# A hybrid attention layer: the first two output tiles' turned planes loaded a step earlier and ahead of their gate rows, and two weight pieces split in one step

## The chip, the cores and the metric

The kernel runs on one core of a Trainium2 chip. What counts is the device time of one launch in microseconds (us). The engines are TensorE (PE; PEld is its weight load), VectorE (DVE), ScalarE (ACT), GpSimd (POOL) and SyncE (SP), which here only issues transfers.

## What is computed

```python
h = rms_norm(x, g_pre) * (1 + scale) + shift          # x: 2048 x 1024, f32
qa, ka, va, fa, za, qb, kb, vb, zb = split(h @ w_in)
oa = forgetting_attention(qa, ka, va, fa + b_fgate)    # 8 heads of 64, causal, with a cumulative gate bias
oa = oa * silu(za)
ob = sliding_window_sink_attention(rope(qb), rope(kb), vb, sinks) * silu(zb)
y = concatenate([oa, ob]) @ w_out                      # 1024 x 1024
out = x + gate * rms_norm(y, g_post)
```

The gate, scale and shift come from `silu(c) @ w_ada + b_ada`.

## The kernel before

Matrix products keep f32 accuracy with f16 operands: each operand is split into a high and a low half, and three matmuls (high x high, high x low, low x high) make one product.

After the projections and the sliding-window branch, the kernel goes through the eight heads of the forgetting attention (`hd` 0 to 7), with 20 steps each (`r` 0 to 19). A step is two key blocks against one chunk of 512 queries; the four chunks take 2, 4, 6 and 8 steps. Step `r` does, in this order: `exp32` on ScalarE (L1354); a tick; `low` of the step before on VectorE (L1365); half of the filler work on TensorE; its own `high` on ScalarE (L1362); the scores of the next step on TensorE (L1349, L1350); a second tick; `pv`, the product with the values of step `r - 2`, on TensorE (L1375 to L1378); the other half of the filler. On the last step of a chunk, `pv` also empties its accumulator on VectorE (L1382, L1384), and some ticks later the result is stored in DRAM as `o_d` (L1388, on SyncE's queue). POOL clears the masked part of diagonal blocks (L1358).

The program order is written out by hand: every engine and every queue works its own instructions in the order in which the code issues them, and waits where data is missing. `after(n, f)` puts `f` off by `n` ticks, so two ticks are one step.

In the last head (`hd` 7) the filler is first the rest of the gate projection (L335, whose results go to `z_d` in DRAM by L378 and L386), and from `r` 11 on the output product. For this product:

- `w_out_load(m)` loads one of 16 pieces of `w_out` (128x512 f32, 256 KB, L1459); `w_out_split(m)` makes its high half (ScalarE L1465 or POOL L1467), `w_out_low(m)` its low half (VectorE L1471). `w_at` says in which step a piece is split; it is loaded three steps before.
- `Out(t)` is an output tile of 128 rows, t = 0 to 15. `load_o` reads the attention planes (high and low half) from `o_d`, turned by the DMA engine (two transposes, L1487), `load_z` the gate rows from `z_d` (512 KB, L1493). Tile t uses the slots `t % 2` of one buffer.
- `turn(lag)` registers a tile's chain: `join` adds the planes (VectorE, L1505, tile `osum`), `gate` multiplies by the gate rows (VectorE, L1509), `squares_` (ScalarE, L1512), `scale_` sums them over partitions on TensorE (L1516) and makes a scale (VectorE, L112, L113), then the high half (ScalarE, L1523) and the low half (VectorE, L1526, tile `oz`) of the product's operand.
- `product` does three matmuls of a unit (L1542). Units come in the order tile 0, tile 1 on the first 512 columns, both on the second, then tiles 2 to 15. Tiles 0 to 3 are partly done between the steps of the last head; the rest of the product runs alone, from step 19's end to the end of the kernel.
- When both column halves of a tile are done, VectorE and ScalarE normalise (L1550, L1564, L92 to L106, L1602) and POOL's queue stores the rows (L1603).

Of the kernel before, what the change touches and what calls it, by code (L numbers as in the profile page):

```python
# [40 lines left out]
def hybrid_layer(  # L41
# [38 lines left out]
    def sm(n, tag):  # L80
        return small.tile([P, n], F32, tag=tag, name=tag)
# [27 lines left out]
    def root_scale(dst, ss):  # L109

        h = small.tile([P, 1], I32, tag="rs_h", name="sc_h")
        V.tensor_scalar(h[:], ss.bitcast(I32), 1, None, op0=ALU.logical_shift_right)  # L112
        V.tensor_scalar(dst.bitcast(I32), h[:], -1, 0x5F3759DF + (15 << 23), op0=ALU.mult, op1=ALU.add)  # L113
# [57 lines left out]
    def bank(hold=False):  # L171
        n = next(n for n in order_ if n not in held)
        order_.remove(n)
        order_.append(n)
        if hold:
            held.add(n)
        return n
# [8 lines left out]
    lag = [0]  # L186

    def after(n, f):
        late.append([n, f])

    def tick():
        now = [f for n, f in late if n <= 1]
        late[:] = [[n - 1, f] for n, f in late if n > 1]
        for f in now:
            f()
# [227 lines left out]
    def turn(ci, k):  # L423

        px = ps_x.tile([P, CH], F32, tag="x", name="px")
        for u in range(4):
            PE.transpose(px[:, u * P:(u + 1) * P], xt[ci * 4 + u][:, k * P:(k + 1) * P], ident[:])
        hf = hst.tile([P, CH], F32, tag="hf", name="hf")
        hi, lo = hT[ci][:, 0, k, :], hT[ci][:, 1, k, :]

        high = k % 2 == 0 if ci else k in (0, 4)

        def scaled():
            for dst in ([hi] if high else []) + [hf[:]]:
                A.activation(dst, px[:], AF.Identity, scale=Gp[:, k:k + 1], bias=Shp[:, k:k + 1])

        def split():
            if not high:
                V.tensor_copy(hi, hf[:])
            V.tensor_tensor(lo, hf[:], hi, op=ALU.subtract)  # L440

        return scaled, split
# [673 lines left out]
    def tick2():  # L1116
        cnt[0] += 1
        if cnt[0] % 2 == 0:
            tick()
# [354 lines left out]
    class Out:  # L1474
# [20 lines left out]
        def turn(self, lag):  # L1495

            self.hl = wpool.tile([P, 2, KT, P], F16, tag=("whl", "wraw")[self.t % 2], name="oz")
            self.sc = sm(1, "w_pw")
            hi, lo = self.hl[:, 0], self.hl[:, 1]
            gs = sm(1, "w_mx")  # L1500

            c = oio["c"]

            def join():
                V.tensor_tensor(c, self.o[:, 0], self.o[:, 1], op=ALU.add)  # L1505
                self.joined = True

            def gate():
                V.tensor_tensor(self.z, c, self.z, op=ALU.mult)  # L1509

            def squares_():
                A.activation(oio["j"][0].rearrange("p (k n) -> p k n", k=KT), self.z, AF.Square, accum_out=gs[:])  # L1512

            def scale_():
                pg = bk[bank()][:, 0:1]
                PE.matmul(pg, ones[:], gs[:], start=True, stop=True)  # L1516
                root_scale(self.sc[:], pg)

            after(1, join)
            after(2 if lag > 4 else 1, gate)  # L1520
            after(3 if lag > 4 else 2, squares_)
            after(lag, scale_)
            after(lag + 1, lambda: A.activation(hi, self.z, AF.Copy, scale=self.sc[:]))  # L1523

            def low():
                V.scalar_tensor_tensor(lo, self.z, self.sc[:], hi, op0=ALU.mult, op1=ALU.subtract)  # L1526
                self.turned = True

            after(lag + 2, low)
# [75 lines left out]
    outs = [Out(t) for t in range(NB)]  # L1605
# [32 lines left out]
    with tc.manual_schedule():  # L1638
        mi = 0
        V.memset(cmask[:], 0.0)  # L1640
        V.tensor_copy(cmask[:, 3 * P:], dmask[:])
        for n in range(2):
            for slot in (2, 0):
                const_rows(n, slot)
                tick()
        fill(8, tick2)
        key_limbs(0)
        key_rows(0)
        tick()
        while pos[0] < N_V3 or mi < M_LEAD:  # L1650
            if pos[0] < N_V3:
                fill(1)
            if mi < M_LEAD and pos[0] >= N_QK0 - 10:
                munits[mi]()
                mi += 1
            tick2()
        for _ in range(3):
            tick()
        steps[0].scores()
        p0, p_one = pos[0], len(punits) - P_LAST - 8  # L1660
        p_tot = p_one + 16 - p0 - P_LEAD
        m_ramp, m_from, m_done = 0, 6 * NS + 7, 7 * NS + 3

        w_at = {3: [0], 4: [1], 5: [2], 6: [3], 7: [4], 8: [5], 10: [6], 11: [7], 12: [8], 13: [9], 14: [10, 11],
                15: [12, 13], 16: [14], 17: [15]}
        w_all = sum(s.w for s in steps[:7 * NS])
        w_acc = 0
        lag[0] = 4
        for s, stp_ in enumerate(steps):
            hd, r = divmod(s, NS)  # L1670
            w_acc += stp_.w
            npn = p0 + P_LEAD + p_tot * w_acc // w_all
            npn = min(npn, (npn + p_one) // 2) - pos[0]
            fil = fill
            if hd == 7:
                npn = len(punits) - P_LAST + min((P_LAST * (r + 1) + 10) // 11, P_LAST) - pos[0]
            if hd == 7 and r > 10:
                npn, fil = N_IN * (r - 10) // (NS - 11) - opos[0], ofill
            m_goal = M_LEAD + int(round((s + 1) * M_HEAD / NS))
            if s == m_from:  # L1680
                m_ramp = mi
            if s >= m_from:
                m_goal = m_ramp + (len(munits) - m_ramp) * (s + 1 - m_from) // (m_done + 1 - m_from)
            m_goal = min(len(munits), m_goal)
            todo = []
            nmn = m_goal - mi
            a = b = 0
            while a < npn or b < nmn:
                if b >= nmn or (a < npn and a * nmn <= b * npn):
                    todo.append(lambda: fil(1))  # L1690
                    a += 1
                else:
                    todo.append(munits[mi + b])
                    b += 1
            mi = m_goal
            half = (len(todo) + 1) // 2
            if r == 2 and hd + 1 < 8:
                key_limbs(hd + 1)
            if hd == 7 and r:
                for m in w_at.get(r + 3, []):  # L1700
                    w_out_load(m)
            stp_.exp32()
            tick()
            if s:
                steps[s - 1].low()
            if hd == 7:
                for m in w_at.get(r, []):
                    w_out_split(m)
            for u in todo[:half]:
                u()  # L1710
            stp_.high()
            if s + 1 < len(steps):
                steps[s + 1].scores()
            tick()
            if s >= PV_LAG:
                steps[s - PV_LAG].pv()
            if hd == 7:
                for m in w_at.get(r, []):
                    w_out_low(m)
            for u in todo[half:]:  # L1720
                u()
            if r == 3 and hd + 1 < 8:
                key_rows(hd + 1)
            if hd == 7 and r == 0:
                open_out()
            if hd == 7 and r == 0:
                for m in w_at[3]:
                    w_out_load(m)
            if hd == 7 and r in (4, 5):
                outs[r - 4].load_z()  # L1730
            if hd == 7 and r in (6, 7):
                outs[r - 6].load_o()
            if hd == 7 and r in (7, 9):
                outs[(r - 7) // 2].turn(5)
            if s % 4 == 1 and s // 4 <= 32:
                w_square(s // 4)
            if s == 134:
                w_sum()
            if s == 136:
                w_root()  # L1740
            if s % 8 == 2 and s // 8 < KT + 2:
                gate_load(s // 8)
            if s % 8 == 7 and s // 8 < KT + 2:
                gate_use(s // 8)
        assert pos[0] == len(punits) and mi == len(munits) and opos[0] == N_IN and not events
        tick()
        steps[-1].low()
        for n in range(PV_LAG, 0, -1):
            steps[-n].pv()
        tick()  # L1750
        tick()
        fxs.close()
        ofill(len(ounits) - opos[0], tick2)
        for _ in range(4):
            tick()
# [35 lines left out]
```

## Time and profile before

| what | us |
|---|---|
| median of 3 runs | 1145.53 |
| lowest, highest | 1144.94, 1145.73 |
| the profiled execution | 1143.33 |
| its span, first to last instruction | 1141.6 |
| busy in it: TensorE, VectorE, ScalarE, POOL | 1101.9, 936.1, 691.8, 252.7 |
| its mean granted TensorE clock | 0.995 of full |

The profile is of one execution; its times are from the start of the span. A row of a timeline gives start, duration, engine, line, operation, result and operands with their shapes, and in brackets how long the engine had been idle and what ended that. A row of waits gives who waited for whom, us in total, times, and the longest. A row of the chain that ended last gives start, duration and what. The mapping of rows to steps follows from the order above: the exponent of step 9 of the last head, for example, is the L1354 at 936.88 us.

### The profile page before, as it was taken

Reading aid. Unit: us, or ns where it says so; the run is one execution under the profiler, and the core shown is the slowest. Engines: PE = TensorE matmul, PEld = TensorE weight load, DVE = VectorE, ACT = ScalarE, POOL = GpSimd, SP = SyncE. Lnnn points to the kernel's source line nnn. Section 1 sums busy time; section 2 is a strip of 40 time slices with the busy share of each in tenths; the row PEclk is TensorE's granted clock in tenths of the full one; section 3 lists DMA queues with packets and bytes.
Section 4 is the critical chain, followed back from the end, with each engine's and each line's share of the span. In section 5 each row is a group of like instructions: output and inputs, shape, how many; then the busy total and the mean of one; then the engine's idle time right before and its main releaser. Section 6 shows DMA issues by size and latency. Waiting matters only on the chain. (4 is left out here: it accounts for less than half of the span.)

```text
span 1141.6 us, 26966 instructions
## 1 busy us (share of the span) xinstructions
PE 1101.9 (97%) x10386; PEld 637.4 (56%) x10386; DVE 936.1 (82%) x2331; ACT 691.8 (61%) x1177; POOL 252.7 (22%) x391
## 2 busy tenths in 40 slices
PE   5899999999999999999999999999999998999997
PEld 1466657654569955555555555555555554544443
DVE  6775668879899658889898889978888988888885
ACT  4676446656666534767767677777777777433331
POOL 2011122434443311122221221202111136100000
PEclk9999999999999999999999999999999999999999
DMA  9646436676787532243332432223212168478753
GB/s 332 225 139 170 105 72 138 113 157 127 158 163 139 115 66 70 68 104 74 81 78 66 103 84 62 59 57 80 61 38 58 25 169 221 133 187 217 189 164 111
DMA packets 210324, 136.35 MB, mean 119 GB/s; under 512 B 145276, under 2 KB 189348, under 8 KB 210196
## 3 DMA queue, kind: packets, MB, share of 16 engines
q1 hardware_dynamic: 198100, 98.53, 37.2%
q0 software_dynamic: 11616, 35.58, 11.0%
q8 instruction: 81, 1.33, 0.5%
q10 hardware_dynamic: 480, 0.53, 0.2%
q14 instruction: 47, 0.39, 0.1%
HBM read 62.58 MB, written 25.18 MB: 77 GB/s over the span
## 5 line engine op out<-in xcount | busy, mean ns | idle before, releaser
L1354 ACT ACTIVATE p<-sta,lift,scl_qk 128x1024 f32<-128x1024 f32 (+2 forms) x160 | 171.8, 1074 | 80.3 <-PE sta L1350 75.8
L335 PE MATMUL bk<-hT,wh_qk 128*128 128x512 f16 x768 | 198.0, 378 | 0.0
L1542 PE MATMUL bk<-hT,oz 128*128 128x512 f16 (+2 forms) x792 | 169.7, 372 | 2.4 <-DVE hT L1471 1.4
L1365 DVE TENSOR_TENSOR pha<-p,pha 128x1024 f16<-128x1024 f32 (+2 forms) x160 | 171.3, 1071 | 0.0
L1362 ACT ACTIVATE pha<-p 128x1024 f16<-128x1024 f32 (+2 forms) x160 | 148.2, 926 | 33.6 <-POOL p L1358 30.0
L1303 DVE TENSOR_REDUCE a_m<-bk 128x1 f32<-128x512 f32 x192 | 129.0, 683 | 33.2 <-PE bk L1300 32.9
L1542 PEld LDWEIGHTS <-oz 128*128 128x128 f16 x792 | 75.9, 99 | 87.7 <-issue 1.7
L1375 PE MATMUL poa<-vt,pha 128*128 128x65 f16 x1088 | 117.2, 193 | 2.1 <-DVE ona L1384 2.1
L1378 PE MATMUL poa<-vt,pha 128*128 128x65 f16 x1088 | 116.6, 193 | 1.8 <-DVE pha L1365 1.7
L1377 PE MATMUL poa<-vt,pha 128*128 128x64 f16 x1088 | 117.0, 195 | 0.0
L1349 PE MATMUL sta<-T 128*128 128x512 f16 (+1 forms) x320 | 109.8, 348 | 3.9 <-ACT p L1354 3.9
L1375 PEld LDWEIGHTS <-pha 128*128 128x128 f16 x1088 | 101.9, 97 | 16.5 <-DVE ona L1384 2.9
L1300 PE MATMUL bk<-T 66*128 66x512 f16 (+2 forms) x320 | 110.2, 348 | 0.8 <-DVE a_m L1305 0.5
L1377 PEld LDWEIGHTS <-pha 128*128 128x128 f16 x1088 | 101.4, 97 | 13.6
L335 PEld LDWEIGHTS <-wh_qk 128*128 128x128 f16 x768 | 70.2, 97 | 69.4 <-issue 0.6
L1350 PE MATMUL sta<-T 69*128 69x512 f16 (+1 forms) x320 | 108.2, 348 | 0.0
L1378 PEld LDWEIGHTS <-pha 128*128 128x128 f16 x1088 | 101.2, 99 | 2.1 <-DVE pha L1365 2.1
L335 PE MATMUL bk<-hT,wh_za 128*128 128x512 f16 x384 | 100.2, 380 | 0.0
L353 PE MATMUL bk<-wh_va,hT 128*128 128x128 f16 x1536 | 92.6, 219 | 0.0
L1358 POOL TENSOR_SCALAR_AFFINE_SELECT p<-p 128x256 f32<-128x256 f32 x64 | 34.7, 542 | 254.9 <-ACT p L1354 234.7
L335 PE MATMUL bk<-hT,wh_zb 128*128 128x512 f16 x384 | 90.8, 379 | 0.0
L353 PEld LDWEIGHTS <-hT 128*128 128x128 f16 x1536 | 87.5, 98 | 4.9 <-issue 2.5
(504 smaller groups left out, 1952.4 us busy)
## 6 DMA issues: line engine op xcount, KB each, us to landing
hT<-in_x_dram SPq DMA_DIRECT2D x20, 512.0 KB
wa<-in_w_ada_dram SPq DMA_DIRECT2D x16, 512.0 KB
T<-stq SPq DMA_DIRECT2D x128, 64.0 KB
T<-z_d SPq DMA_DIRECT2D x16, 512.0 KB
out_dram<-hT POOLq DMA_DIRECT2D x15, 512.0 KB, 5.7
z_d<-tz POOLq DMA_DIRECT2D x29, 256.0 KB, 3.1
xt<-in_x_dram SPq DMA_DIRECT2D x12, 512.0 KB
qs<-qf SPq DMA_DIRECT2D x80, 64.0 KB
```

The costliest lines, as they stand in the source:

```text
L335: PE.matmul(ps, whl[:, a, k, :], hT[ci][:, b, k, :], start=(k == 0 and n == 0), stop=(k == KT - 1 and n == 2))
L353: PE.matmul(ps[:, u * P:(u + 1) * P], hT[ci][:, a, k, u * P:(u + 1) * P], whl[:, b, k, :], start=(k == 0 and n == 0), stop=(k == KT - 1 an ...
L1300: PE.matmul(mx[:, :w], T[0:XM, 0, i * P:(i + 1) * P], T[0:XM, 2, pc * CH:pc * CH + w], start=True, stop=True)
L1303: V.tensor_reduce(m3[:, u, pc:pc + 1], mx[:, :w], axis=AX.X, op=ALU.max)
L1349: PE.matmul(self.st[:, o:o + w], T[:, 3, kb_], T[:, 1, qc], start=True, stop=False)
L1354: A.activation(self.p32[:, :self.w], self.st[:, :self.w], AF.Exp, scale=scl[f"qk{self.hd}"][:], bias=lift[:])
L1362: A.activation(self.ph[:, 0, :self.w], self.p32[:, :self.w], AF.Copy)
L1365: V.tensor_tensor(self.ph[:, 1, :self.w], self.p32[:, :self.w], self.ph[:, 0, :self.w], op=ALU.subtract)
L1375: PE.matmul(po[:, u, :], ph[:, 0, pq], vt[:, b, hd, 0:65], start=(self.first and n == 0 and u == 0), stop=False)
L1377: PE.matmul(po[:, u, 0:64], ph[:, 0, pq], vt[:, b, hd, 65:VW], start=False, stop=False)
L1378: PE.matmul(po[:, u, :], ph[:, 1, pq], vt[:, b, hd, 0:65], start=False, stop=(self.last and n == len(self.blocks) - 1))
L1542: PE.matmul(py, self.hl[:, i, k, :], w_piece(8 * j + k, cc), start=(k == 0 and m_ == 0), stop=(k == KT - 1 and m_ == 2))
```

## The change

In the last head the planes of tiles 0 and 1 (`load_o`) are issued at the end of steps 5 and 6 instead of 6 and 7. Their gate rows (`load_z`) move from steps 4 and 5 to 5 and 6, behind the planes. `turn` is called at the end of steps 6 and 8 instead of 7 and 9, with lag 6 instead of 5. Counted in ticks after that call, the chain is now: join 1, gate 2, squares 4, scale 6, high half 7, low half 8; it was 1, 2, 3, 5, 6, 7. So tile 0's join goes from the first tick of step 8 to the first of step 7, its low half from the first tick of step 11 to the second of step 10. Later tiles call `turn(7)`; their order is unchanged.

Piece 15 of `w_out` is split in step 16, with piece 14, instead of step 17. `w_from` keeps every load where it was.

```diff
             after(1, join)
-            after(2 if lag > 4 else 1, gate)
-            after(3 if lag > 4 else 2, squares_)
+            after(2, gate)
+            after(4 if lag == 6 else 3, squares_)
             after(lag, scale_)
...
         w_at = {3: [0], 4: [1], 5: [2], 6: [3], 7: [4], 8: [5], 10: [6], 11: [7], 12: [8], 13: [9], 14: [10, 11],
-                15: [12, 13], 16: [14], 17: [15]}
+                15: [12, 13], 16: [14, 15]}
+        w_from = {m: (13 if m == 14 else 14 if m == 15 else r - 3) for r, ms in w_at.items() for m in ms}
...
             if hd == 7 and r:
-                for m in w_at.get(r + 3, []):
+                for m in (m for m, at in w_from.items() if at == r):
                     w_out_load(m)
...
-            if hd == 7 and r in (4, 5):
-                outs[r - 4].load_z()
-            if hd == 7 and r in (6, 7):
-                outs[r - 6].load_o()
-            if hd == 7 and r in (7, 9):
-                outs[(r - 7) // 2].turn(5)
+            if hd == 7 and r in (5, 6):
+                outs[r - 5].load_o()
+                outs[r - 5].load_z()
+            if hd == 7 and r in (6, 8):
+                outs[(r - 6) // 2].turn(6)
```

## The prediction

> **What bounds the kernel now.** I read the page first (busy shares, the chain that ended last), then the waits between 880 and 990 us, then each engine's timeline there.
>
> ```profile
> PE 1101.9 (97%) x10386; PEld 637.4 (56%) x10386; DVE 936.1 (82%) x2331; ACT 691.8 (61%) x1177; POOL 252.7 (22%) x391
> ...
> 987.38 12.97 PE bk L1542 x60
> ...
> DVE osum L1505 <- DMA T<-o_d: 2.7, 1, 2.7
> PE poa L1378 <- DVE pha L1365: 1.7, 2, 1.4
> PE sta L1349 <- ACT p L1354: 1.7, 2, 0.9
> PE bk L1542 <- DVE hT L1471: 1.4, 1, 1.4
> PE bk L1542 <- DVE oz L1526: 0.7, 1, 0.7
> ```
>
> TensorE is the bound. From 987.38 us (second line, from the chain) it streams the output product with nothing to wait for, and no line of that stretch is edited. So the change is worth exactly what it shifts that 987.38. Before it, the four TensorE waits shown come to 5.5 us. The first line, VectorE's 2.7 us for the turned planes, comes ahead of all but the one for L1471.
>
> **The first two tiles' chain: when do the planes land?** This is SyncE's queue, in order. L1388 stores the last head's first rows to o_d, L1493 loads a gate tile (512 KB), L1459 a w_out piece (256 KB), L1487 the two transposes of a tile (start, duration of the issue).
>
> ```profile
> 927.60 0.40 SPq L1388 DMA_DIRECT2D o_d<-oha  x1
> 928.04 0.57 SPq L1493 DMA_DIRECT2D T<-z_d  x1
> 928.71 0.56 SPq L1459 DMA_DIRECT2D hT<-in_w_out_dram  x1
> 929.32 0.42 SPq L1493 DMA_DIRECT2D T<-z_d  x1
> 930.26 6.38 SPq L1487 DMA_TRANSPOSE T<-o_d  x2
> ...
> 937.32 3.08 SPq L1487 DMA_TRANSPOSE T<-o_d  x2
> 982.11 3.57 SPq L1487 DMA_TRANSPOSE T<-o_d  x2
> ...
> SPq L1487 <- DMA o_d<-oha: 0.5, 1, 0.5
> ```
>
> The code moves load_o a step earlier, but the transposes read what L1388 wrote: SyncE was already at them and waited 0.5 us for that store. So tile 0's pair cannot begin before about 930.26, a step sooner or not. What does change is the load ahead of it. Now 1.25 MB (two gate tiles, one w_out piece) stand in front and the pair takes 6.38 us to issue; afterwards only the 256 KB piece does. The bounds for the pair are 3.08 us (tile 1's) and 6.38. I take 3.1, the low end, because 3.08 is also behind one w_out piece; 3.57 had a gate tile ahead. The planes land 2.02 us after the issue ends (936.64 to VectorE's join at 938.66, below). So: 930.26 + 3.1 + 2.0 = 935.4 instead of 938.66, 3.3 us sooner.
>
> **What that is worth on VectorE.** These are VectorE's rows (start, duration, idle before). L1505 is the join, L1509 the gate, L1526 the low half of the product's operand, L1365 the low half of an attention step, L1471 a w_out low piece, L1382/L1384 the last attention rows of a query chunk.
>
> ```profile
> 930.93 1.18 DVE L1471 SCALAR_TENSOR_TENSOR hT<-wo,wsc,hT 128x512 f16<-128x512 f32 x1
> 933.57 0.69 DVE L378 SCALAR_TENSOR_TENSOR gz<-gz,bk 128x512 f32<-128x512 f32 x1 [0.33 <-ACT gz L388]
> 934.64 0.18 DVE L1382 RECIPROCAL a_ri<-poa 128x4 f32<-128x4 f32 x1 [0.38 <-PE poa L1378]
> 934.86 0.42 DVE L1384 TENSOR_TENSOR ona<-poa,a_ri 128x256 f32<-128x256 f32 x1
> 938.66 1.22 DVE L1505 TENSOR_TENSOR osum<-T 128x1024 f32<-128x1024 f16 x1 [2.71 <-DMA T<-o_d]
> 939.80 1.22 DVE L1365 TENSOR_TENSOR pha<-p,pha 128x1024 f16<-128x1024 f32 x1
> 940.93 1.22 DVE L1509 TENSOR_TENSOR T<-osum,T 128x1024 f32<-128x1024 f32 x1
> 942.07 0.74 DVE L1471 SCALAR_TENSOR_TENSOR hT<-hT,wsc,hT 128x512 f16<-128x512 f32 x1
> 943.87 0.15 DVE L112 TENSOR_SCALAR sc_h<-bk 128x1 int32<-128x1 int32 x1
> 946.41 1.43 DVE L1509 TENSOR_TENSOR T<-osum,T 128x1024 f32<-128x1024 f32 x1
> 948.82 1.28 DVE L1526 SCALAR_TENSOR_TENSOR oz<-T,w_pw,oz 128x1024 f16<-128x1024 f32 x1 [0.32 <-ACT oz L1523]
> ...
> 936.61 0.19 PE L1375 MATMUL poa<-vt,pha 128*128 128x65 f16 x1
> 937.35 1.46 PE L335 MATMUL bk<-hT,wh_za 128*128 128x512 f16 x6
> 950.16 1.04 PE L1542 MATMUL bk<-hT,oz 128*128 128x512 f16 x4 [0.70 <-DVE oz L1526]
> ```
>
> The join moves from the first tick of step r=8 to that of r=7, so it now stands right behind the L1471 that ends at 932.1 (930.93 + 1.18), ahead of that step's L1365. VectorE stops there and waits to 935.4: 3.3 us, longer than the 2.71 that goes, though it ends sooner. Behind it are queued, by the new order and by start-to-start distances in the rows above (join 1.14, L1365 1.13, gate 1.14): join to 936.5, L1365 to 937.7, L378 0.6 to 938.3, gate to 939.4, L1382 and L1384 0.6 to 940.0, L1471 0.7 to 940.7, L1365 to 941.8, L1471 to 942.5, tile 1's join to 943.6, L1365 to 944.7, the two root steps 0.3 to 945.0, tile 1's gate 1.35 (946.41 to the next start) to 946.3, L1365 to 947.4, then L1526 ends at 948.7. That is 13.3 us without a gap. The product's first matmul that needs it runs at 948.76 instead of 950.16: **1.4 us gained**, less than the 3.3 by which the planes come sooner, because four more instructions (an L1365, L378, L1382, L1384) now lie between join and L1526.
>
> Do the others keep up? TensorE's attention product at 936.61 needs the accumulator that L1384 empties, so it stops from 936.6 to 940.1, a new gap of 3.5 us. Then come 0.74 of that product (936.61 to 937.35) and six L335 at 0.216 each (the pace of 12.97 over 60), to 942.15. By the same paces another 4.8 us of scores, attention and three units bring it to the output product near 946.9. ScalarE:
>
> ```profile
> 936.88 1.19 ACT L1354 ACTIVATE p<-sta,lift,scl_qk 128x1024 f32<-128x1024 f32 x1
> 942.19 1.06 ACT L1512 ACTIVATE hT<-T 128x1024 bf16<-128x1024 f32 x1 [4.12 <-DVE T L1509]
> 946.79 0.95 ACT L1362 ACTIVATE pha<-p 128x896 f16<-128x896 f32 x1 [0.91 <-POOL p L1358]
> 947.65 1.13 ACT L1523 ACTIVATE oz<-T,w_pw 128x1024 f16<-128x1024 f32 x1
> ```
>
> The squares (L1512) now stand ahead of the exponent of step 9 (with lag 6, second tick of r=8): they start at 939.5, when the gate is done, and with 1.06, a small copy of some 0.4 and 1.19 that exponent ends at 942.1 (its row today: 936.88). The scores that wait for it stand at 942.15 on TensorE, so this delay hides in the new gap. L1523 can start once the root steps are done at 945.0, and is over before VectorE needs it at 947.4; today it comes at 947.65, behind L1362 and POOL's select. TensorE, there at 946.9, waits for VectorE, whose sum decides. From 950.16 to 975 the orders are the same but for tile 1's chain, half a step earlier, on which no wait shown hangs; the shift is carried.
>
> **The gate rows** are moved behind the transposes. They are issued near 933.8 and needed at 938.3. Their 512 KB follow the planes at 935.4; at the 260 GB/s below that is 2.0 us, 937.4, and 938.4 if they share with half of tile 1's planes: 0 to 0.1 us, taken as nothing.
>
> ```profile
> 946.00:948.00 2.00, 2.00 (x27) 1.41 (x24) 2.00 (x3) 1.21 (x2) 0.76 (x1) 0.50 0.42 150
> 952.00:956.00 4.00, 4.00 (x54) 2.54 (x53) 2.54 (x6) 3.51 (x4) 3.96 (x4) 1.00 1.13 260
> ```
>
> **The clock** is the 0.50 in the first of these rows (last three columns: granted clock, DMA share, GB/s). TensorE's waits just before are those of the first list, none over 1.4 us. It costs nothing today: the 950.16 start hangs on the ScalarE and VectorE rows, not on TensorE. After the new 3.5 us gap it can cost more, as TensorE is then busy from 940.1 to 946.9: a stretch of 2 to 4 us at half clock loses 1 to 2 us there, and 948.7 - 946.9 = 1.8 of it is slack. What passes the slack or delays VectorE's root steps I put at 0 to 0.4, taken 0.1.
> The Trainium skill, "TensorE: Matmul & The Clock Gate", Part 1, has the clock halved after a whole idle window of about 3.4 us. The row disagrees, since no gap before it was half as long. By the page a 3.5 us gap would rarely cover a window and the 0.1 would be nothing; by the row the halving is nearly sure.
>
> **The split.** No load moves (w_from keeps 13 and 14), only piece 15's split and low half, from step 17 to 16.
>
> ```profile
> 963.71 8.73 POOL L1467 TENSOR_SCALAR hT<-hT,wsc 128x512 f16<-128x512 f32 x4
> 975.89 0.16 DVE L112 TENSOR_SCALAR sc_h<-bk 128x1 int32<-128x1 int32 x1 [1.34 <-PE bk L1516]
> 977.30 0.89 DVE L1471 SCALAR_TENSOR_TENSOR hT<-hT,wsc,hT 128x512 f16<-128x512 f32 x1
> 978.25 1.89 PE L1542 MATMUL bk<-hT,oz 128*128 128x512 f16 x8 [1.43 <-DVE hT L1471]
> 986.18 0.55 DVE L1365 TENSOR_TENSOR pha<-p,pha 128x384 f16<-128x384 f32 x1
> ```
>
> POOL runs pieces 12 to 15 back to back already, done at 972.44, so nothing changes there. VectorE's low half fits before 975.89, where it waits 1.34 us. TensorE's wait of 1.43 goes. But what is late next is VectorE: from 975.89 to the last L1365 at 986.18 it has no gap, and the last attention product before 987.38 waits for that L1365. Out of that row of work comes one L1471, 0.82 us at most; the bounds are 0 and 1.43, and I take 0.75.
>
> **Sum:** -1.4 - 0.75 + 0.1 = -2.05. The profiled execution took 1143.33 us (span 1141.6); it becomes 1141.3. The median of the runs is 1145.53, 2.2 above it, so 1143.5.
>
> **Rivals.**
> *The pair stays slow* (slower). If 6.38 is the price of tile 0's pair for another reason than the gate tiles (its first issue took most of it, and POOL's store runs beside it), the planes land at 938.66 again, now ahead of 13.3 us of VectorE work: L1526 ends at 952.0, 1.8 later than now, less 0.75: +1.1, 1146.6, up to 1147.0 with the half clock. Every us of landing is a us; with the split, a landing after 937.5 makes it a loss. For it speaks that no pair free of load stands at this place; against it the 3.08.
> *A quick pair:* 2.8 us and landing at 934.9, clock unharmed: -2.7, 1142.8.
> *Only the split pays:* the planes land near 936.8: -0.75, 1144.8.
> *Gate rows late:* past 938.3 each us is one; the gain is gone at 940.4: 1145.5. It needs 6.6 us for one gate tile.
>
> **How the numbers follow.** Measurement tells 0.2%, 2.3 us, from no change, so the forecast lies at the edge. Forecast (landing 934.9 to 935.9) 0.5, with -2.5 to -1.5, of which 0.18 is faster; quick pair or more from the split 0.25, all faster; split alone or gate rows late 0.10, same; slow pair 0.15, of which 0.10 passes 2.3 us with further delays. That gives faster 0.43, same 0.47, slower 0.10. The range takes in the quick pair with the whole 1.43 of the split (1142.1) and the slow pair (1146.6).
>
> **What would show it.** Right: first L1487 pair at about 930.3 for 3.1 us; first L1505 at 935.4 after 3.4 us of idle; a TensorE gap of 3.5 us near 937 to 940 released by L1384; first L1526 ends by 948.7; no wait of L1542 for L1471; the 12.97 us run starts at 985.3. Wrong: a pair of 5 us or more, a first L1509 that waits for z_d, or a last L1365 that has not moved.

## The result, and the profile after

| kernel | median, us | lowest to highest | runs |
|---|---|---|---|
| before | 1144.99 | 1142.82 to 1149.21 | 22 |
| changed | 1143.12 | 1141.26 to 1145.21 | 22 |

The ratio is 0.9985, with a 95% interval of 0.9979 to 0.9991: the change saves 1.87 us by the medians. The forecast was 1143.5 us and -2.05. The total came out near the forecast; its two halves did not come out as the forecast had them, as the rows show. The page of the changed kernel (busy us), its chain of work that ended last, and its waits between 880 and 990 us:

```profile
PE 1100.5 (96%) x10386; PEld 636.9 (56%) x10386; DVE 938.9 (82%) x2331; ACT 691.8 (61%) x1177; POOL 251.5 (22%) x391
```

```profile
987.35 12.97 PE bk L1542 x60
```

```profile
PE poa L1375 <- DVE ona L1384: 3.5, 1, 3.5
DVE osum L1505 <- DMA T<-o_d: 3.4, 1, 3.4
...
PE poa L1378 <- DVE pha L1365: 1.0, 1, 1.0
```

PE's waits for L1471 (1.4) and for the low half L1526 (0.7) are gone from the list, and the new wait for L1384 stands on top of it. VectorE's wait at the join has grown from 2.7 to 3.4. Yet the run of 60 matmuls starts at 987.35, where it started at 987.38. The two profiled executions did not reach the last head's end at the same time: the store L1388, which no part of the change touches, is at 928.53 now and was at 927.60. So I count from that store, here and below. The stretch from it to the run of 60 was 59.78 us (987.38 - 927.60) and is 58.82: 0.96 less.

The timelines of the changed kernel (SyncE's queue, VectorE, TensorE; start, duration, in brackets the idle time before and what ended it), and its granted clock (third column from the end of the second fence):

```profile
928.53 0.39 SPq L1388 DMA_DIRECT2D o_d<-oha  x1
928.98 0.57 SPq L1459 DMA_DIRECT2D hT<-in_w_out_dram  x1
930.86 2.69 SPq L1487 DMA_TRANSPOSE T<-o_d  x2
933.60 0.57 SPq L1493 DMA_DIRECT2D T<-z_d  x1
...
937.17 1.23 DVE L1505 TENSOR_TENSOR osum<-T 128x1024 f32<-128x1024 f16 x1 [3.38 <-DMA T<-o_d]
...
939.45 0.68 DVE L378 SCALAR_TENSOR_TENSOR gz<-gz,bk 128x512 f32<-128x512 f32 x1
940.05 1.22 DVE L1509 TENSOR_TENSOR T<-osum,T 128x1024 f32<-128x1024 f32 x1
...
941.39 0.42 DVE L1384 TENSOR_TENSOR ona<-poa,a_ri 128x256 f32<-128x256 f32 x1
...
943.53 1.16 DVE L1471 SCALAR_TENSOR_TENSOR hT<-hT,wsc,hT 128x512 f16<-128x512 f32 x1
944.61 1.21 DVE L1505 TENSOR_TENSOR osum<-T 128x1024 f32<-128x1024 f16 x1
...
949.61 1.27 DVE L1526 SCALAR_TENSOR_TENSOR oz<-T,w_pw,oz 128x1024 f16<-128x1024 f32 x1
...
941.87 0.20 PE L1375 MATMUL poa<-vt,pha 128*128 128x65 f16 x1 [3.46 <-DVE ona L1384]
...
950.24 1.73 PE L1542 MATMUL bk<-hT,oz 128*128 128x512 f16 x6
```

```profile
942.00:944.00 2.00, 2.00 (x28) 1.17 (x27) 2.00 (x3) 1.97 (x5) 1.11 (x1) 0.68 1.04 370
944.00:946.00 2.00, 2.00 (x6) 0.69 (x5) 2.00 (x3) 0.94 (x1) 0.69 (x2) 0.50 0.59 169
```

The pair is issued in 2.69 us, quicker than forecast. But the join starts 3.62 us after the issue has ended (930.86 + 2.69 = 933.55), where it was 2.02 before. And L1526 ends at 950.88, which is 22.35 after the store; before it was 22.50 (948.82 + 1.28 - 927.60). So the early planes brought the operand 0.15 us forward. Nearly all of the 0.96 is elsewhere.

### The profile page after: what moved, and what is told of

It reads as the page before. It is cut to its first block, busy times and chain, and to the rows that moved or that the text cites. A ratio compares the mean times of both kernels' runs of the same rounds, so it can differ in the third digit from the quotient of the medians.

```text
span 1141.6 us, 26965 instructions
## 1 busy us (share of the span) xinstructions
PE 1100.5 (96%) x10386; PEld 636.9 (56%) x10386; DVE 938.9 (82%) x2331; ACT 691.8 (61%) x1177; POOL 251.5 (22%) x391
## 4 chain that ended last, share of the span: by engine, by line
PE 73%; DVE 13%; ACT 5%; issue 4%; DMA 4%; SPq 1%; POOL 1%; DVEq 0%; ACTq 0%; POOLq 0%
PE bk L335 27%; PE bk L1542 13%; PE bk L353 6%; PE sta L1349 4%; PE bk L1300 4%; PE sta L1350 4%; PE poa L1377 2%; PE poa L1378 2%; PE poa L1375 2%; DMA wa<-in_w_ada_dram 2%; DVE pha L1365 2%; PE bk L779 1%; DVE a_m L1303 1%; PE pss L873 1%; PE pob L936 1%
## 5 line engine op out<-in xcount | busy, mean ns | idle before, releaser
L1354 ACT ACTIVATE p<-sta,lift,scl_qk 128x1024 f32<-128x1024 f32 (+2 forms) x160 | 171.9, 1074 | 81.4 <-PE sta L1350 77.1
L1365 DVE TENSOR_TENSOR pha<-p,pha 128x1024 f16<-128x1024 f32 (+2 forms) x160 | 171.7, 1073 | 0.0
L1362 ACT ACTIVATE pha<-p 128x1024 f16<-128x1024 f32 (+2 forms) x160 | 148.2, 926 | 33.6 <-POOL p L1358 30.0
L1377 PEld LDWEIGHTS <-pha 128*128 128x128 f16 x1088 | 101.0, 97 | 13.3
```

Source lines behind the costliest of these rows:

```text
L1354: A.activation(self.p32[:, :self.w], self.st[:, :self.w], AF.Exp, scale=scl[f"qk{self.hd}"][:], bias=lift[:])
L1362: A.activation(self.ph[:, 0, :self.w], self.p32[:, :self.w], AF.Copy)
L1365: V.tensor_tensor(self.ph[:, 1, :self.w], self.p32[:, :self.w], self.ph[:, 0, :self.w], op=ALU.subtract)
L1377: PE.matmul(po[:, u, 0:64], ph[:, 0, pq], vt[:, b, hd, 65:VW], start=False, stop=False)
```

## The experiments

My theory after the result: the split pays about 0.75 as forecast, and the chain pays almost nothing, because its planes land later than the sum had them and because more of VectorE's and TensorE's work now stands behind the join. The rival: the chain pays the 1.4 of the forecast, and the one profiled execution doesn't show it. Each ratio is to the kernel before on the same chip. e1 to e4 ran on one chip, e5 to e8 on a second and e9 to e12 on a third, so ratios of different groups are only roughly comparable. Each column of times is one profiled execution; e9 and the changed kernel, which should agree, differ by 0.25 us in the last. e10, further down, ran once, for its profile alone. The table counts in us from the store L1388 (step 4) of each profile, to the start of tile 0's pair of transposes, of the first join, of the first L1526, and of the run of 60.

| kernel | ratio to before (95%) | pair | join | L1526 | run of 60 |
|---|---|---|---|---|---|
| before | 1 | 2.66 | 11.06 | 21.22 | 59.78 |
| changed | 0.9985 (0.9979 to 0.9991) | 2.33 | 8.64 | 21.08 | 58.82 |
| e1_split_only | 0.9992 (0.9983 to 1.0) | 2.68 | 11.14 | 21.12 | 59.00 |
| e2_chain_only | 0.9999 (0.9990 to 1.0008) | 2.45 | 8.96 | 21.79 | 60.50 |
| e3_gate_rows_first | 0.9999 (0.9990 to 1.0008) | 2.38 | 9.38 | 21.82 | 59.55 |
| e4_old_chain | 0.9980 (0.9971 to 0.9988) | 2.42 | 8.56 | 19.19 | 56.94 |
| e5_piece_behind | 0.9986 (0.9977 to 0.9994) | 2.36 | 8.20 | 21.29 | 59.21 |
| e6_loads_only | 0.9982 (0.9972 to 0.9991) | 2.36 | 8.98 | 19.61 | 59.67 |
| e7_turn4 | 0.9958 (0.9944 to 0.9971) | 2.34 | 9.08 | 17.31 | 56.73 |
| e8_ticks | 0.9953 (0.9941 to 0.9966) | 2.34 | 8.60 | 17.05 | 54.79 |
| e9_busy_gap | 0.9987 (0.9979 to 0.9996) | 2.46 | 8.59 | 20.82 | 58.57 |
| e11_ticks_old_loads | 0.9971 (0.9961 to 0.9982) | 2.71 | 11.08 | 19.04 | 56.78 |
| e12_ticks_piece_behind | 0.9961 (0.9947 to 0.9975) | 2.46 | 8.26 | 18.63 | 56.38 |

**The change in two halves.** e1 is the kernel before with only this of the change (and the loop that reads `w_from`); e2 is the changed kernel without it.

```diff
-                15: [12, 13], 16: [14], 17: [15]}
+                15: [12, 13], 16: [14, 15]}
+        w_from = {m: (13 if m == 14 else 14 if m == 15 else r - 3) for r, ms in w_at.items() for m in ms}
```

> The kernel before with the split of piece 15 alone moved to step 16. Theory A (both parts pay: the chain 1.1 us, the split 0.75, because the last attention product then waits longer for VectorE): 0.75 us faster than before, with TensorE's 1.43 us wait for L1471 gone and its wait for the last L1365 grown from 0.26 to about 0.9. Theory B (the whole gain is the split's, the chain only moves its wait): 1.9 us faster.

> The changed kernel without the moved split: loads and chain of the first two tiles alone. Theory A: 1.1 us faster than before, with the wait of 1.4 us for L1471 still there. Theory B: no change, the join's wait of 2.7 us being replaced by one of 3.4 us on VectorE and one of 3.5 us on TensorE.

Rows of e1 (SyncE's queue, TensorE, and its chain that ended last), then of e2 (the same, and a row of VectorE):

```profile
929.15 0.40 SPq L1388 DMA_DIRECT2D o_d<-oha  x1
...
987.57 0.20 PE L1378 MATMUL poa<-vt,pha 128*128 128x65 f16 x1 [1.04 <-DVE pha L1365]
```

```profile
988.15 12.97 PE bk L1542 x60
```

```profile
927.18 0.39 SPq L1388 DMA_DIRECT2D o_d<-oha  x1
...
946.22 0.16 DVE L112 TENSOR_SCALAR sc_h<-bk 128x1 int32<-128x1 int32 x1 [0.30 <-PE bk L1516]
...
940.84 0.24 PE L1375 MATMUL poa<-vt,pha 128*128 128x65 f16 x1 [4.48 <-DVE ona L1384]
...
978.55 1.89 PE L1542 MATMUL bk<-hT,oz 128*128 128x512 f16 x8 [1.43 <-DVE hT L1471]
```

```profile
987.68 12.97 PE bk L1542 x60
```

The split alone shortens the stretch by 0.78 us and the time by a ratio of 0.9992. The chain alone has the planes 2.1 us sooner, and gains nothing: its first L1526 starts 0.57 later than before, TensorE stands 4.48 us at the accumulator, and the ratio is 0.9999. So e1 came out where its theory A has the split, and e2 where its theory B has the chain; neither of the two theories holds for both. Against the rival above: a chain that pays 1.4 us would give e2 0.9988, which lies outside its interval. In the profiles what the change saves is about the split's worth, as my theory has it; by time alone e1's interval reaches 1.0.

e2's operand is 0.71 later after the store than the changed kernel's, with the same loads and chain: its join came 0.32 later, and VectorE stood 0.30 at the root steps (L112), waiting for L1516 on a TensorE that had half clock from 938.8 to 945.6. So what the chain does varies from execution to execution, between -0.15 (changed) and +0.57 (e2).

**The order of the loads.** e3 is the changed kernel with the two calls swapped:

```diff
-                outs[r - 5].load_o()
                 outs[r - 5].load_z()
+                outs[r - 5].load_o()
```

> The changed kernel with each tile's gate rows issued ahead of its planes, in the same steps. Theory A (the planes' landing counts one to one, and what is issued ahead of them delays it): 512 KB ahead make the pair's issue about 1.5 us longer, the join starts 1.5 us later and the kernel is 1.5 us slower than the changed one, near the time before. Rival C (the pair starts only when the store has landed, and the gate rows flow in that time): at most 0.5 us slower than the changed kernel.

```profile
926.41 0.39 SPq L1388 DMA_DIRECT2D o_d<-oha  x1
...
928.79 4.89 SPq L1487 DMA_TRANSPOSE T<-o_d  x2
...
935.79 1.23 DVE L1505 TENSOR_TENSOR osum<-T 128x1024 f32<-128x1024 f16 x1 [4.87 <-DMA T<-o_d]
```

With 512 KB more ahead, the pair takes 4.89 us to issue instead of 2.69, but the join comes only 0.74 later after the store (9.38 against 8.64), and the stretch is 0.73 longer. Between these two executions a later landing passes on us for us, as the prediction had it; e5, below, does not follow that. The join's 0.74 lies between theory A's 1.5 and rival C's 0.5. The ratio is 0.9999, the time before, as theory A has it, though its interval just overlaps that of the changed kernel: without the order of the loads the change's gain can't be told from nothing.

**How long does a landing take?** e5 issues the 256 KB w_out piece of step 5 behind the planes and gate rows (first diff). e10 loads only one of tile 0's two planes (second).

```diff
-                for m in (m for m, at in w_from.items() if at == r):
+                for m in (m for m, at in w_from.items() if at == r and r != 5):
...
                 outs[r - 5].load_z()
+                if r == 5:
+                    w_out_load(5)
```

```diff
-            for a in range(2):
+            for a in range(1 if t == 0 else 2):
...
-                V.tensor_tensor(c, self.o[:, 0], self.o[:, 1], op=ALU.add)
+                V.tensor_tensor(c, self.o[:, 0], self.o[:, 1 if self.t else 0], op=ALU.add)
```

> The changed kernel, but the w_out piece that step 5 loads (256 KB, L1459, issued between the store L1388 and tile 0's pair of L1487) is issued behind the planes and gate rows instead. In the changed kernel the join (L1505) ended its wait 8.64 us after the store's issue, 3.6 us after the pair's issue had ended. Theory A, the planes land late because the piece's bytes run ahead of them and beside them: the join comes at 7.6 to 8.1 us after the store, TensorE's wait for L1384 falls from 3.46 to 2.5-3.0, and the time is 0.4 to 1.0 us under that of the changed kernel (about 2.3 to 2.9 us under the kernel before, ratio near 0.9977). Rival B, the landing is the transposes' own pace: the join stays at 8.4 to 8.8, the wait at 3.3 to 3.6, the time within 0.3 us of the changed kernel (ratio 0.9984).

> The changed kernel, but tile 0 loads only the first of its two turned planes, and the join adds that plane to itself (the output's first 128 rows are computed from half the value). For the landing alone. In the changed kernel the pair's issue took 2.69 us and the join could start 6.31 us after its beginning, 3.6 after its end. Theory A, the planes land at the pace of their bytes through the transposition: one plane is there 3.2 to 4.0 us after its issue begins, VectorE's wait at the join falls from 3.4 to under 1.2. Rival B, a fixed delay of some 3.6 us follows the end of the issue: 1.35 + 3.6 = 4.7 to 5.2 us, wait 1.7 to 2.5.

e10's queue and VectorE:

```profile
929.87 1.29 SPq L1487 DMA_TRANSPOSE T<-o_d  x1
...
935.63 1.23 DVE L1505 TENSOR_TENSOR osum<-T 128x1024 f32<-128x1024 f16 x1 [3.65 <-DMA T<-o_d]
```

Both theories of e10 miss, in its one execution. One plane takes 1.29 us to issue and its join can start 5.76 us after the issue began, hardly sooner than two planes (6.31 in the changed kernel), and 4.47 after the issue ended. So neither the bytes of the pair nor a fixed delay after the issue sets the landing alone. Counted from the beginning of the pair's issue to the join, the runs sort by what was issued on SyncE's queue just ahead of the pair: 5.84 with no piece (e5); 6.13 to 6.74 behind 256 KB (changed, e2, e4, e6 to e9); 7.00 behind 768 KB (e3); 8.37 to 8.46 behind 1.25 MB (before, e1, e11). What spreads the 256 KB group by 0.6 us is open. e5's 0.44 us of earlier landing lies between its two theories, and is worth nothing in time (0.9986 against 0.9985, perhaps on another chip), as rival B has it. Its profile shows where it went: its first L1526 starts later than the changed kernel's (21.29 against 21.08), and VectorE waited for L1516 there, behind a TensorE that had half clock from 938.9 to 945.7:

```profile
946.29 0.16 DVE L112 TENSOR_SCALAR sc_h<-bk 128x1 int32<-128x1 int32 x1 [0.37 <-PE bk L1516]
```

**The join at its old place.** e4 is the changed kernel with its loads and split, but with `turn(5)` at the end of steps 7 and 9 as before; e6 undoes e4's split too, so that only the loads differ from the kernel before.

```diff
-            if hd == 7 and r in (6, 8):
-                outs[(r - 6) // 2].turn(6)
+            if hd == 7 and r in (7, 9):
+                outs[(r - 7) // 2].turn(5)
```

> The changed kernel's loads and split with the chain as before (turn at the end of steps 7 and 9, lag 5), so that the join stands one step after the place it has in the changed kernel. Theory A (what costs is VectorE standing still in order behind the join): the join's wait falls from 3.4 us to under 1 us, TensorE's gap of 3.5 us goes, and the kernel is about 1.8 us faster than the changed one, 3 us faster than before. Rival D (the earlier chain is what pays): slower than the changed kernel by about 1 us, as the product's first operand is ready half a step later.

> The kernel before with nothing but the planes and gate rows loaded as in the changed kernel (steps 5 and 6, planes first); chain at its old place, split at its old step. With the split as well this gave 56.94 us from the store L1388 to the last run of 60 matmuls L1542, against 59.78 before and 0.9980 in time. Theory A, the early landing pays by itself, since it takes away VectorE's wait at the join and with it TensorE's gap: about 57.7 us, 2.0 under before, less the split's 0.8: time -1.0 to -1.6 us, ratio 0.9986 to 0.9991. Rival B, the early landing only lets the split pay in full (1.43, what the product waited for the piece): stretch 59 us or more, ratio 0.9995 to 1.0.

Rows of e4, then the granted clock of e4 and of e6 in the same two microseconds:

```profile
936.35 1.23 DVE L1505 TENSOR_TENSOR osum<-T 128x1024 f32<-128x1024 f16 x1 [0.21 <-DMA T<-o_d]
...
947.00 0.61 PE L1542 MATMUL bk<-hT,oz 128*128 128x512 f16 x2 [1.63 <-ACT oz L1523]
948.32 1.04 PE L1542 MATMUL bk<-hT,oz 128*128 128x512 f16 x4 [0.71 <-DVE oz L1526]
```

```profile
948.00:950.00 2.00, 1.68 (x8) 0.80 (x9) 2.00 (x4) 2.00 (x5) 2.00 (x2) 1.00 0.19 40
```

```profile
948.00:950.00 2.00, 1.66 (x4) 0.58 (x5) 2.00 (x3) 2.00 (x5) 2.00 (x2) 0.50 0.20 37
...
952.00:954.00 2.00, 2.00 (x26) 1.26 (x23) 0.69 (x3) 1.97 (x3) 1.96 (x3) 1.00 1.17 231
```

Left at its old place, the join meets planes that are there almost at once (0.21 us of waiting), VectorE does its L1365, L1382 and L1384 first, and TensorE has no gap at the accumulator. The first L1526 then starts at 19.19, 2.0 us sooner than before. This is the gain that the prediction looked for; the change had the planes for it, but moved the join so far forward that VectorE waited for them. By time this is not settled against the changed kernel: the intervals of e4 and the changed kernel overlap, and e4 stays short of theory A's 3 us (0.9980 is 2.3). Against e2 and e3, on the same chip, its interval lies below theirs. e6, with the loads alone and without the split, has 0.9982, as much as the whole change; that is a larger saving than theory A's 0.9986 to 0.9991, a range within e6's interval, and it rules out rival B. Its profiled stretch, 59.67, fits B instead: that execution had TensorE at half clock from 948 to 951, right in the output product. From the product's start behind L1526 to its next group of three it took 3.97 us (948.34 to 952.31), e4 2.48: 1.49 of the stretch, without which it would be 58.18, near theory A's 57.7.

**The half clock behind the gap.** e9 puts 14 unused matmuls into the changed kernel's gap:

```diff
+            if hd == 7 and r == PV_LAG + 6:
+                pd = bk[bank()]
+                for _ in range(14):
+                    PE.matmul(pd[:], w_piece(0, slice(0, P)), w_piece(0, slice(0, CH)), start=True, stop=True)
```

> The changed kernel with 14 matmuls more (128x512 f16 into a free bank of PSUM, result unused, some 3.0 us) on TensorE right before the attention product that waits 3.46 us for L1384, so that TensorE is busy in that gap. In the changed kernel's profile the granted clock fell to 0.50 from 942.7 to 946.4 behind the gap. Theory A, the halved clock came from the gap and only used up slack, since VectorE's L1526 ends last: the clock stays at 1.00 there, the product's third matmul still waits for L1526, and the time is that of the changed kernel, ratio 0.9978 to 0.9988. Rival B, the halving is what ate the 1.4 us: 0.9 to 1.6 us less than the changed kernel, ratio 0.9965 to 0.9977. Rival C, the halving has another cause than the gap: clock 0.50 again near 943, time unchanged.

```profile
936.30 3.18 PE L1719 MATMUL bk<-hT 128*128 128x512 f16 x14
...
949.44 1.04 PE L1542 MATMUL bk<-hT,oz 128*128 128x512 f16 x4 [1.57 <-DVE oz L1526]
```

```profile
942.00:944.00 2.00, 2.00 (x26) 1.34 (x25) 2.00 (x3) 1.97 (x3) 1.40 (x2) 1.00 0.85 305
944.00:946.00 2.00, 2.00 (x28) 1.27 (x25) 1.97 (x5) 0.73 (x2) 1.11 (x1) 1.00 0.99 258
```

With the gap filled the clock stays at 1.00, TensorE is early and waits 1.57 us for L1526, and the time is that of the changed kernel (0.9987). So in these two executions the halving came with the gap, and it only used up slack: VectorE's chain sets the product. It is not free in every execution: in e2 and e5, where it lasted twice as long, VectorE waited 0.30 and 0.37 us for L1516, as shown above.

**A shorter chain.** If the chain's length binds, the way is to shorten it, not to start it early. e7 is e4 with `turn(4)` (scale, high and low half one tick sooner: squares 3, scale 4, high half 5, low half 6); e8 has squares at tick 4, scale and high half at 5, low half at 6. e11 is e8 with the loads of the kernel before; e12 is e8 with e5's edit. (In e8, e11 and e12 the product is L1543 and the low half L1527.) Against e4, e7 is the first line, and e8 all:

```diff
-                outs[(r - 7) // 2].turn(5)
+                outs[(r - 7) // 2].turn(4)
...
-            after(4 if lag == 6 else 3, squares_)
+            after(4 if lag in (4, 6) else 3, squares_)
+            lag += lag == 4
             after(lag, scale_)
-            after(lag + 1, lambda: A.activation(hi, self.z, AF.Copy, scale=self.sc[:]))
+            after(lag + (lag != 5), lambda: A.activation(hi, self.z, AF.Copy, scale=self.sc[:]))
...
-            after(lag + 2, low)
+            after(lag + 2 - (lag == 5), low)
```

> Early loads, split in one step, the join at its old place (end of steps 7 and 9), but scale, high and low half one tick sooner than in the old chain (lag 4: join 1, gate 2, squares 3, scale 4, high 5, low 6). With lag 5 the stretch from L1388 to the last run of 60 L1542 took 56.94 us and TensorE still waited 1.63 for L1523 and 0.71 for L1526 (first product). Theory A, these two waits are the chain's length: they go, stretch 55.5 to 56.3, ratio 0.9970 to 0.9976. Rival B, the engines before it are full: the squares and the high half push ScalarE's exponents or VectorE's L1365, whose waits on TensorE grow by as much: stretch 56.7 to 57.3, ratio 0.9978 to 0.9984.

> As the run with lag 4, but squares at tick 4, scale and high half both at tick 5, low half at tick 6: the squares stand behind the next exponent on ScalarE and the scale keeps its old tick. Theory A (the waits for L1523 and L1526 are the chain's length): they go as with lag 4, stretch 55.3 to 56.3, ratio 0.9968 to 0.9976, and no worse than lag 4. Rival B: the high half has no time between the root steps and its own tick, ScalarE waits for w_pw by 1 us or more ahead of it and the exponents behind it come as late as before: stretch 56.7 to 57.3, ratio 0.9978 to 0.9984.

> The run e8_ticks (join at the end of steps 7 and 9, squares tick 4, scale and high half tick 5, low half tick 6, split in one step; ratio 0.9953) with the loads where the kernel before has them: gate rows at steps 4 and 5, planes at 6 and 7. Theory A, the short chain pays only with the early planes, since the join waits 2.7 us for the late ones and everything behind it is later by that: 2.0 to 3.0 us above e8_ticks, ratio 0.9973 to 0.9985. Rival B, the gain is that of the ticks alone and the wait at the join hides elsewhere: ratio 0.9950 to 0.9965.

> The run e8_ticks with the w_out piece of step 5 issued behind the planes and gate rows. In e8_ticks the join still waits 0.26 us for the planes; alone with the changed kernel the move brought the landing 0.44 us closer to the store. Theory A: the 0.26 goes and no more, 0 to 0.4 us under e8_ticks, ratio 0.9948 to 0.9955. Rival B, the join is no longer what decides and the piece, split on POOL at step 8, is late: ratio 0.9955 to 0.9970.

e8's timelines and chain that ended last, then e11's, and a row each of e7 and of e12:

```profile
927.07 0.40 SPq L1388 DMA_DIRECT2D o_d<-oha  x1
...
935.67 1.23 DVE L1505 TENSOR_TENSOR osum<-T 128x1024 f32<-128x1024 f16 x1 [0.26 <-DMA T<-o_d]
...
945.45 1.04 PE L1543 MATMUL bk<-hT,oz 128*128 128x512 f16 x4 [1.27 <-DVE oz L1527]
```

```profile
981.86 12.97 PE bk L1543 x60
```

```profile
927.63 0.39 SPq L1388 DMA_DIRECT2D o_d<-oha  x1
...
938.71 1.23 DVE L1505 TENSOR_TENSOR osum<-T 128x1024 f32<-128x1024 f16 x1 [2.55 <-DMA T<-o_d]
```

```profile
984.41 12.97 PE bk L1543 x60
```

```profile
942.55 0.38 PE L1516 MATMUL bk<-w_mx,ones 128*128 128x1 f32 x2 [2.31 <-ACT hT L1512]
```

```profile
941.21 1.15 DVE L1471 SCALAR_TENSOR_TENSOR hT<-hT,wsc,hT 128x512 f16<-128x512 f32 x1 [1.47 <-POOL hT L1467]
```

e8 is the fastest of all: 1138.85 us median (1137.79 to 1140.32), ratio 0.9953, beyond theory A's best and below the kernel before and the changed one; its stretch is 5.0 us shorter than before. Its squares stand behind the step's L1362 and ahead of the next exponent (L1362 at 937.57, L1512 at 939.68, L1354 at 940.74), not behind that exponent as the expectation has it. e7's time is under theory A's too (0.9958), though its profiled stretch, 56.73, is rival B's: it has a 2.31 us gap at the first L1516 and half clock behind it, as lag 4 brings L1516 half a step forward on TensorE, ahead of an attention product, while the squares that it needs stay where they were. e11, with late planes and 2.55 us of waiting at the join, still has 0.9971, a little better than theory A's 0.9973, which its interval includes: of e8's gain about six tenths (0.0029 of 0.0047 in the ratios, 3.00 of 4.99 us in the stretches) are the ticks and the split, the rest the early planes. e12 came out at 0.9961, in the range of rival B, where e8 has 0.9953; the intervals overlap, so its time doesn't decide. Its profile shows rival B's mechanism: the join no longer waits, but POOL splits the delayed piece only at 939.30 (11.58 after the store; in e8 at 931.89, 4.82 after it), VectorE's L1471 waits 1.47 us for that, and the first L1527 starts 1.58 later than in e8.

## Why the prediction was right in the sum and wrong in its parts

*TensorE's last run is the bound, and the change is worth what it shifts it.* Right. Over the table the stretch and the ratio rise and fall together, roughly; furthest off is e6, whose profile had the half clock in the product.

*The pair's start and issue: 2.66 after the store, 3.1 us.* Right, and on the safe side, in this execution: 2.33 and 2.69. With the same transfers ahead, e4, e9 and e2 took 3.78, 3.81 and 4.15 us to issue the pair, and their joins came as early (8.56, 8.59, 8.96): the issue alone says little about the landing.

*Landing 2.02 us after the issue ends.* **This step failed.** I carried a delay measured behind a slow issue (6.38) over to a quick one. It was 3.62: what shrinks is the issue, and the landing shrinks less. Over the runs, a pair issued in 2.64 to 3.05 us was in use 3.20 to 3.73 after the issue, one issued in 3.78 us or more 2.01 to 2.36 after it. The join came 8.64 after the store, not 7.8: 0.84 of the gain lost.

*VectorE then works 13.3 us without a gap.* The order and the absence of gaps were right. It took 13.71 (937.17 to 950.88): one L1471 took 1.08 to the next start (943.53 to 944.61), not 0.7, though the prediction's own rows had L1471 at 0.74 and at 1.18. Another 0.41, nearly all of it from that row. So of the **1.4 us** remained 1.4 - 0.84 - 0.41 = 0.15, which is the 0.15 that L1526's rows show. The rival "only the split pays" (planes near 936.8) told the mechanism: on the prediction's clock the landing is 936.2 (937.17 less the 0.93 by which this execution was late), and the 0.41 does the rest.

*A TensorE gap of 3.5 us behind L1384.* Right: 3.46.

*Half clock after the gap, nearly sure, in the slack.* Right, but nearer to the edge than forecast: 0.50 from 944 to 946, and e9 shows that no time hung on it. TensorE reached the product at 949.3 on the prediction's clock instead of 946.9 and L1526 ended at 949.95; the third matmul needs that, so some 0.2 us of slack was left (an estimate: 949.95 less 949.3 and two matmuls of 0.216). The 0 to 0.4 that the halving could cost at the root steps came true in e2 and e5. The prediction weighed the Trainium skill, "TensorE: Matmul & The Clock Gate", Part 1, which asks for a whole idle window. In these profiles every gap of 2.31 us or more brought the half clock (changed kernel, e2, e3, e5, e7, e10), but it also came in the kernel before and in e1 and e6, whose longest gap was 1.64, and it stayed away in e12 with 1.70. The rows disagree with a whole idle window of 3.4 us as the condition. What decides among the short gaps is told in the last section.

*Gate rows cost nothing behind the planes.* Right: the first gate (L1509) ran at 940.05 behind L378, with no wait.

*The split, -0.75.* Right: e1 shows -0.78. The wait of 1.43 went, and what was late next was the last L1365, as forecast: TensorE's wait for it is 1.04 in e1 and in the changed kernel.

*Sum.* -0.15 - 0.78 = -0.93, against -0.96 of the two profiles and -2.05 forecast. The medians say -1.87, and the interval of the ratio reaches from -1.0 to -2.4 (0.9991 and 0.9979 of 1145 us). So the median agrees with the forecast better than the forecast's working does, and that agreement is luck as far as the profiles go. The two halves run alone, e1 and e2, multiply to 0.9991, the edge of that interval; whether the rest of the 1.87 is a gain that these profiled executions don't show stays open.

## What to carry to other kernels

When an operand is made ready sooner, move its consumer only as far as the landing allows: on an engine that works in program order, a consumer that comes up too early holds up everything behind it, and the other engines with it. Here the early loads paid about 2 us with the join left alone (e6, 0.9982) and nothing with the join moved (e2, 0.9999; the two intervals just touch). And look at the length of the whole chain before the start of it: one tick taken out of the middle shortened the stretch by as much as the early loads did (2.15 us from e4 to e8, 1.99 from e11 to e8).

## What the runs showed of the hardware

The issue time of a pair of transposes and the time until its data can be used don't add as two fixed pieces. Issue took 2.64 to 6.43 us, from its beginning to use 5.84 to 8.46, and the slower issue had the smaller remainder (e1: 6.43 and 2.03; e5: 2.64 and 3.20). Half the data (e10, one execution) still took 5.76.

The half clock comes in one execution and not in the next for almost the same program (e6 and e4), and where it falls on the product it costs 1.5 us, most of what the change itself saves. The traces show what decides. From 10 to 1120 us of all fourteen profiles it lasts 3.41 us or twice that, and inside one execution its beginnings and ends lie whole multiples of 3.413 us apart, to within 0.02 (before: 27.30, 30.71, 945.48 and 948.89). So each execution can be cut into windows of 3.413 us, where the last head has no half clock counted on from the one near 27 us that every profile has.

At full clock, the halving always came behind a window in which TensorE was busy, by the profile, for 1.56 us or less (46% of it, e1), and never behind one of 1.76 us or more (changed kernel, at 280 us). In between lie two windows of 1.72 us: the one before the kernel before's half clock, and one of e12 that none followed. Once halved, the clock stayed so behind windows of up to 3.05 us busy (89%, e10) and came back behind those of 3.07 us or more (e6), so the edge for coming back lies near nine tenths. In e6 the window ahead of the product was busy for 1.40 us, in e4 the least busy one of the last head for 1.78. So a gap of 1.5 us can bring the half clock or not, by where it falls on windows whose position differs from execution to execution.
